# Depthwise convolution by spectra over tokens, with the way back in plain float32

## The chip, the cores and the metric

The kernel runs on one core of a Trainium2 chip. What counts is the device time of one execution in microseconds (us). The engines are PE (TensorE, matrix products into PSUM), DVE (VectorE), ACT (ScalarE), POOL (GpSimd) and SP (SyncE, whose queue here issues every DMA). A line number such as L288 is a line of the kernel file.

## The reference

Two transformer blocks on 256 tokens of 1024 features in float32. The change touches one layer of the second block only, the conformer convolution:

```python
def conformer_conv(h, w_pw1, b_pw1, w_dw, b_dw, ln_g, ln_b, w_pw2, b_pw2):
    u = h @ w_pw1 + b_pw1                 # 256x1024 by 1024x2048
    a, gate = jnp.split(u, 2, axis=-1)
    u = a * jax.nn.sigmoid(gate)
    u = causal_dwconv_2(u, w_dw, b_dw)    # 31 taps over tokens, each feature by itself
    u = jax.nn.silu(layernorm(u, ln_g, ln_b))
    return u @ w_pw2 + b_pw2              # 1024x1024
# second_block: h = rmsnorm_2(x, ...);  x = x + conformer_conv(h, ...)
```

## The kernel before

All weights stream from DRAM in blocks of 128 x 1024 floats (0.52 MB). `chunk` loads one into a `raw` buffer (5 of them, SP's queue), ACT copies it to a rounded `hi` part (L335), and DVE subtracts that for a `lo` part (L336; 7 buffers of each). A product of full precision is three products of parts, high by high, high by low and low by high. `mm_b` does this with features on PSUM's partitions and 256 tokens as columns; `mm_a` with 128 tokens on the partitions and features as columns. `mm` (L288) is the one line behind all of them, so names of tiles tell products apart. Plain float32 products go through the same `mm`.

A framework with tile pools puts the semaphores and the order in which each engine takes its work; in this stage the order of steps is written out by hand in a string (`CONV_ORDER`).

The stage runs thus. The 256 tokens stand along columns, the features on partitions. `up_pair("pw1", j)` makes for each of 8 feature tiles the value and the gate half of the first pointwise layer, 16 blocks, 384 products of 256 columns (`ps_pw`). `glu` scales by the input's norm (`rsb`), adds biases, and writes `u` with 31 columns of zeros ahead (`upad`). Of the 31 taps some are multiply-adds on DVE (`conv_dve`, L948, 66 of them). The others run on PE: `conv_rows` sends the rows out to DRAM (`far`, L953) and reads them back with four shifted copies over the partitions (`ur`, L957), POOL builds diagonal matrices from the taps (`dw`), and `conv_pe` makes 184 products of 32 output rows (`pcv`). `PW_PE` says how many of eight groups of taps PE takes for each tile. Mean and variance over features are products with a matrix of ones (`pmu`, `pvar`, `pmd`), then the rest of the norm, SiLU, the split into parts, and the second pointwise layer (`pw`, 8 blocks, 192 products). The gated feed-forward behind it begins with `ps_up`.

The norm of the stage's input comes in the middle of the first products: `nm.row` sums squares with three products (`ssa`, `ssb`) and gives `rsb`. `tok_col` turns such a row into a column of scales by token (`ps_col`).

Of the kernel before, what the change touches and what calls it, by code (L numbers as in the profile page):

```python
# [56 lines left out]
def _plan():  # L57
# [87 lines left out]
def _dve_taps():  # L145

    return [(j, k) for j in range(8) for k in range(31) if (k + 1) % 8 >= PW_PE[j]]


def _rows4(w):  # L150

    w = np.concatenate([np.zeros_like(w[:1]), w], axis=0).reshape(4, 8, 8, 4, 32)
    return w.transpose(0, 4, 2, 1, 3).reshape(P, 256)
# [12 lines left out]
def _w2(w):  # L166
# [20 lines left out]
    ("b_pw1", 16, lambda I: _col(I["conv_b_pw1_2"], 16)),  # L187
    ("w_dw", 256, lambda I: _rows4(I["conv_w_dw_2"][0])),
    ("w_dv", len(_dve_taps()), lambda I: _taps(I["conv_w_dw_2"][0], 8)[:, [31 * j + k for j, k in _dve_taps()]]),
    ("b_dw", 8, lambda I: _col(I["conv_b_dw_2"], 8)),  # L190
# [18 lines left out]
def _offsets(items):  # L209
    o, out = 0, {}  # L210
    for name, n, *_ in items:
# [8 lines left out]
         ("cos", T), ("sin", T), ("cmpadd", 64), ("cmpmul", 64), ("eye4", 32), ("sbmask", P), ("cmask", P)]  # L220
# [46 lines left out]
def kernel(ctx: ExitStack, tc: tile.TileContext, x: bass.AP, mem: bass.AP, stream: bass.AP,  # L267
# [653 lines left out]
    yc = apool.tile([P, ND, T], F32, tag="b8", name="yc")  # L921
    NH = 31
    dve_taps = _dve_taps()

    def glu(j, ps):

        rt(rs)
        ag = spool.tile([P, 2, T], F32, tag="t2", name="ag", bufs=NT2)
        dve.tensor_mul(ag, ps, rb(rs))
        sg = spool.tile([P, T], F32, tag="t1", name="sg", bufs=NT1)  # L930
        fn(sg, ag[:, 1, :], AF.Sigmoid, bias=vec("b_pw1", 8 + j))
        up = spool.tile([P, NH + T], F32, tag="t1", name="upad", bufs=NT1)
        pool.memset(up[:, 0:NH], 0.0)
        dve.scalar_tensor_tensor(up[:, NH:], ag[:, 0, :], vec("b_pw1", j), sg, op0=ALU.add, op1=ALU.mult)
        return up

    def conv_dve(*js):

        first = {j: max([t for t in dve_taps if t[0] == j], default=None) for j in js}
        for k in range(30, -1, -1):  # L940
            for j in js:
                if (j, k) not in dve_taps:
                    continue
                w, u = vec("w_dv", dve_taps.index((j, k))), ups[j][:, k + 1:k + 1 + T]
                if (j, k) == first[j]:
                    act.activation(yc[:, j, :], u, AF.Identity, scale=w, bias=vec("b_dw", j))
                else:
                    dve.scalar_tensor_tensor(yc[:, j, :], u, w, yc[:, j, :], op0=ALU.mult, op1=ALU.add)  # L948

    def conv_rows(up):  # L950

        far = dpool.tile([P, NH + T], F32, tag="far", name="far")
        nc.sync.dma_start(far, up)  # L953
        r = apool.tile([P, 4, T + 7], F32, tag="c4", name="ur", bufs=NC4)
        for b in range(4):
            f = far[32 * b:32 * b + 32]
            nc.sync.dma_start(r[:, b, :], bass.AP(f.tensor, f.offset, [[8, 4], [NH + T, 32], [1, T + 7]]))  # L957
        return r

    def conv_pe(j):  # L960

        ps = acc_bank([P, T], "pcv")
        n = PW_PE[j]
        d = wpool.tile([P, 8, 4, 32], F32, tag="lo", name="dw", bufs=7)
        src = vec("w_dw", 32 * j, 4 * n).rearrange("p (g b) -> p g b", b=4)
        pool.tensor_mul(d[:, :n], src[:, :, :, None].to_broadcast([P, n, 4, 32]),
                        con("eye4")[:, None, None, :].to_broadcast([P, n, 4, 32]))
        for g in range(n):
            for b in range(4):
                mm(ps[32 * b:32 * b + 32, :], d[:, g, b, :], uss[j][:, b, g:g + T], g == 0, g == n - 1)  # L970
        return ps

    def conv_sum(j, ps):
        if PW_PE[j] == 8:
            act.activation(yc[:, j, :], ps, AF.Identity, bias=vec("b_dw", j))
        else:
            dve.tensor_add(yc[:, j, :], ps, yc[:, j, :])


    ups, uss, pcs, pss, w4, ln = {}, {}, {}, {}, [], {}  # L980

    def conv_mean():
        pmu = ms_bank([P, T], "pmu")
        m = spool.tile([P, T], F32, tag="t1", name="yp", bufs=NT1)
        pool.tensor_add(m, yc[:, 0, :], yc[:, 1, :])
        for i, y in enumerate((m, yc[:, 2, :], yc[:, 3, :])):
            mm(pmu, ones, y, i == 0, i == 2)
        ln["mu"] = spool.tile([P, T], F32, tag="t1", name="mu", bufs=NT1)
        act.activation(ln["mu"], pmu, AF.Copy, scale=1.0 / (4 * P))
        ln["var"], ln["md"] = up_bank([P, T], "pvar"), ms_bank([P, T], "pmd")  # L990

    def deviate(p):
        s = slice(2 * p, 2 * p + 2)
        dve.tensor_sub(yc[:, s, :], yc[:, s, :], rb(ln["mu"]))

    def moments(js):
        sq = spool.tile([P, 2, T], F32, tag="t2", name="sq", bufs=NT2)
        act.activation(sq[:, 0:len(js), :], yc[:, js[0]:js[-1] + 1, :], AF.Square)
        y = yc[:, js[0], :]
        if len(js) == 2:  # L1000
            pool.tensor_add(sq[:, 0, :], sq[:, 0, :], sq[:, 1, :])
            if js[0] == 4:
                y = spool.tile([P, T], F32, tag="t1", name="yp", bufs=NT1)
                pool.tensor_add(y, yc[:, 4, :], yc[:, 5, :])
        if js[0] >= 4:
            mm(ln["md"], ones, y, js[0] == 4, js[0] == 7)
        mm(ln["var"], ones, sq[:, 0, :], js[0] == 0, js[0] == 7)

    dve_groups = ((0, 1), (2, 4), (3, 5), (6, 7))

    steps = {
        "P": lambda j: pss.update({j: up_pair("pw1", j, xs, nm.row if j == PW_ORDER[1] else None)}),
        "G": lambda j: ups.update({j: glu(j, pss[j])}),
        "S": lambda j: PW_PE[j] and uss.update({j: conv_rows(ups[j])}),
        "E": lambda j: PW_PE[j] and pcs.update({j: conv_pe(j)}),
        "A": lambda j: PW_PE[j] and conv_sum(j, pcs[j]),
        "D": lambda j: conv_dve(*dve_groups[j]),
        "w": lambda j: w4.append(chunk(("pw2", j), D)),
        "m": lambda j: conv_mean(),
        "d": deviate,  # L1020
        "M": lambda j: moments((j,) if j > 5 else (j, j + 1)),
    }
    for step in CONV_ORDER.split():
        steps[step[0]](int(step[1]))
    m2 = spool.tile([P, T], F32, tag="t1", name="m2", bufs=NT1)
    act.activation(m2, ln["md"], AF.Square, scale=1.0 / math.sqrt(D))
    md = spool.tile([P, T], F32, tag="t1", name="md", bufs=NT1)
    dve.tensor_scalar(md, ln["md"], 1.0 / D, None, op0=ALU.mult)
    dve.tensor_sub(m2, ln["var"], m2)
    rl = rs_of(m2, D, eps2, "rl")  # L1030
    ys = pair_tile("x", bufs=2)
    acc = Acc("pw2")
    for p in range(4):
        s = slice(2 * p, 2 * p + 2)
        dve.tensor_sub(yc[:, s, :], yc[:, s, :], rb(md))
        dve.tensor_mul(yc[:, s, :], yc[:, s, :], rb(rl))
        for f in (2 * p, 2 * p + 1):
            fn(yc[:, f, :], yc[:, f, :], AF.Silu, scale=vec("ln_g", f), bias=vec("ln_b", f))
        for f in (2 * p, 2 * p + 1):
            split(ys, (slice(None), f), yc[:, f, :])  # L1040
        if p < 2:
            acc.add(("pw2", 2 * p), ys, 2 * p, w4[2 * p:2 * p + 2])
# [402 lines left out]
```

## Time and profile before

| | us |
|---|---|
| median of 3 runs | 1069.94 (1069.94, 1071.75, 1069.94) |
| the profiled execution | 1071.3 |
| its span, first to last instruction | 1069.5 |
| PE busy | 1035.4 (97%) |
| DVE busy | 734.8 (69%) |
| ACT busy | 579.7 (54%) |
| POOL busy | 60.2 (6%) |

All rows are from the one profiled execution. Its own time is 1.8 us over the span, and 1.4 us over the median. The mean granted clock of PE was 0.988 of full speed (2.4 GHz).

### The profile page before, as it was taken

To read this page: it belongs to the slowest core of one execution; us is meant where nothing else is said; L and a number is where in the kernel's file an instruction comes from. 1 tells how busy PE (TensorE), PEld (TensorE's weight loads), DVE (VectorE), ACT (ScalarE), POOL (GpSimd) and SP (SyncE) were. 2 spreads that over 40 slices of the span, in tenths; PEclk is the share of its full clock that TensorE was granted. 3 is DMA by queue.
4 is the path that set the end of the run, shared out by engine and by line. 5 is a ranking of instruction groups with operands and counts; after the bars stand their busy time and mean duration, and the time that the engine had idled before them with its cause. 6 is when DMAs were issued, how large, how long until landed. Compare 5 with 4: busy or idle time off the path is not lost.

```text
span 1069.5 us, 20182 instructions
## 1 busy us (share of the span) xinstructions
PE 1035.4 (97%) x8113; PEld 957.5 (90%) x8113; DVE 734.8 (69%) x1163; ACT 579.7 (54%) x968; POOL 60.2 (6%) x148
## 2 busy tenths in 40 slices
PE   7999999999999999778999999999999999999998
PEld 6998898999999999537999999998786799999997
DVE  5976568745545587955876677766887468667673
ACT  5766657644444473215654555553867656555551
POOL 0000000000000000320000000000124300000000
PEclk9999999999999999879999999999999999999999
DMA  8753234355655655352555555644742045656641
GB/s 307 241 182 119 79 119 157 131 186 176 195 182 173 195 168 155 96 165 76 186 187 179 181 189 167 197 156 139 226 139 60 2 126 190 199 177 196 182 154 40
DMA packets 52813, 170.43 MB, mean 159 GB/s; under 512 B 5744, under 2 KB 13168, under 8 KB 52720
## 3 DMA queue, kind: packets, MB, share of 16 engines
q1 hardware_dynamic: 51952, 168.09, 48.8%
q8 instruction: 64, 1.05, 0.4%
q0 software_dynamic: 768, 1.05, 0.4%
q14 instruction: 29, 0.24, 0.1%
HBM read 165.99 MB, written 2.08 MB: 157 GB/s over the span
## 4 chain that ended last, share of the span: by engine, by line
PE 87%; DMA 6%; DVE 5%; ACT 1%; issue 1%; SPq 0%; DVEq 0%; ACTq 0%
PE ps_up L288 23%; PE ff L288 9%; PE ps_ff L288 8%; PE ob L288 6%; PE dn L288 6%; PE ps_v L288 3%; PE nl L288 2%; PE pw L288 2%; PE ps_qk L288 2%; PE no L288 2%; PE wo L288 2%; DMA far<-upad 2%; PE npo L288 2%; DVE yc L948 2%; PE ps_nq L288 2%; DMA ur<-far 2%
## 5 line engine op out<-in xcount | busy, mean ns | idle before, releaser
L336 DVE TENSOR_TENSOR lo<-raw,hi 128x1024 fp32r<-128x1024 f32 x296 | 358.2, 1223 | 169.1 <-ACT hi L335 157.3
L335 ACT ACTIVATE hi<-raw 128x1024 fp32r<-128x1024 f32 x296 | 305.2, 1049 | 261.6 <-PE ps_up L288 62.9
L288 PE MATMUL ps_up<-xh,hi 128*128 128x256 f32 x704 | 199.6, 284 | 0.3 <-DVE fv L1057 0.3
L288 PE MATMUL ps_up<-xl,hi 128*128 128x256 f32 x704 | 199.5, 283 | 0.0
L288 PE MATMUL ps_up<-xh,lo 128*128 128x256 f32 x704 | 199.2, 283 | 0.0
L288 PEld LDWEIGHTS ps_up<-xh,hi 128*128 128x128 f32 x704 | 135.1, 192 | 0.9 <-DVE fv L1057 0.5
L288 PEld LDWEIGHTS ps_up<-xl,hi 128*128 128x128 f32 x704 | 135.1, 192 | 0.4
L288 PEld LDWEIGHTS ps_up<-xh,lo 128*128 128x128 f32 x704 | 135.1, 192 | 0.0
L288 PE MATMUL ff<-us,hi 128*128 128x256 f32 x512 | 92.8, 283 | 0.0
L288 PEld LDWEIGHTS ff<-us,hi 128*128 128x128 f32 x512 | 79.4, 190 | 0.2
L288 PE MATMUL ps_ff<-xh,hi 128*128 128x256 f32 x256 | 72.7, 284 | 0.2 <-DVE fr L871 0.2
L288 PE MATMUL ps_ff<-xl,hi 128*128 128x256 f32 x256 | 72.4, 283 | 0.0
L288 PE MATMUL ps_ff<-xh,lo 128*128 128x256 f32 x256 | 72.4, 283 | 0.0
L288 PE MATMUL ff<-us,lo 128*128 128x256 f32 x256 | 72.1, 282 | 0.0
L288 PE MATMUL dn<-us,hi 128*128 128x256 f32 x352 | 63.5, 282 | 0.0
L288 PE MATMUL ob<-hi,us 128*128 128x512 f32 x176 | 56.2, 392 | 0.0
L288 PEld LDWEIGHTS dn<-us,hi 128*128 128x128 f32 x352 | 54.6, 191 | 0.0
L288 PE MATMUL dn<-us,lo 128*128 128x256 f32 x176 | 49.7, 282 | 0.0
L288 PEld LDWEIGHTS ps_ff<-xh,hi 128*128 128x128 f32 x256 | 49.1, 192 | 0.4 <-PE ps_ff L288 0.4
L288 PEld LDWEIGHTS ps_ff<-xl,hi 128*128 128x128 f32 x256 | 49.1, 192 | 0.0
L288 PEld LDWEIGHTS ps_ff<-xh,lo 128*128 128x128 f32 x256 | 49.1, 192 | 0.0
L288 PEld LDWEIGHTS ff<-us,lo 128*128 128x128 f32 x256 | 48.7, 190 | 0.0
(417 smaller groups left out, 2394.6 us busy)
## 6 DMA issues: line engine op xcount, KB each, us to landing
raw<-in_stream_dram SPq DMA_DIRECT2D x302, 512.0 KB
ur<-far SPq DMA_DIRECT2D x28, 131.5 KB
xin<-in_mem_dram SPq DMA_DIRECT2D x4, 256.0 KB
xin<-in_x_dram SPq DMA_DIRECT2D x4, 256.0 KB
out_dram<-htok SPq DMA_DIRECT2D x4, 256.0 KB
far<-upad SPq DMA_DIRECT2D x7, 143.5 KB
ct<-in_cons_dram SPq DMA_DIRECT2D x1, 720.0 KB
vt<-in_vecs_dram SPq DMA_DIRECT2D x1, 539.0 KB
```

The source lines that it names most:

```text
L288: pe.matmul(ps, l, r, start=start, stop=stop, skip_group_check=True, **kw)
L335: act.activation(hi[:, :width], raw[:, :width], AF.Copy)
L336: dve.tensor_sub(lo[:, :width], raw[:, :width], hi[:, :width].bitcast(F32))
L948: dve.scalar_tensor_tensor(yc[:, j, :], u, w, yc[:, j, :], op0=ALU.mult, op1=ALU.add)
```

## The change

Only the convolution stage changes, up to the products `pw`; those and all that follows are as before. Tokens now lie on the partitions. The first layer is four projections of 512 features (`g0`, `a0`, `g1`, `a1`: gate and value, first and second half), each of four blocks and 48 products of 512 columns (`mm_a`). The biases come as rows broadcast over the partitions by DMA (`bb`, two buffers). The convolution is done in blocks of 128 tokens by a real DFT of length 160: 36 products of parts with a table (`ps_f`), a multiplication with the spectrum of the taps on DVE (`sq`), and 8 plain float32 products back (`ps_y`). The tap spectra are four float32 products with 32 rows (`ps_sp`). The table and the taps are loaded into two of the five `raw` buffers. The layer norm is bn_stats and bn_aggr by token, Ln and Exp for the reciprocal root, one scaling on ACT and one on DVE for each half of the tokens, 16 transposes back to features (`ps_t`), and SiLU. The scratch in DRAM (`far`) is gone, the vectors shrink from 1078 to 727 columns, and the constants lose a small identity.

```diff
@@ the weight stream @@
-    for j in PW_ORDER:
-        both("pw1", "conv_w_pw1_2", 0, j, D)
+    add(("dft", 0), 1024, lambda I: _dft())
+    add(("taps", 0), 256, ...)
+    add(("b_pw1", 0), 16, ...)
+    for b in range(2):
+        wide(("g", b), D + 512 * b)
+        wide(("a", b), 512 * b)
@@ the stage @@
-    glu, conv_dve, conv_rows, conv_pe, conv_sum, conv_mean, deviate, moments
-    for step in CONV_ORDER.split():
-        steps[step[0]](int(step[1]))
-    m2, md, rl, and yc = (yc - md) * rl on DVE
+    def dft_load():
+        raw, _ = raw_chunk(("dft", 0))
...
+        taps = wpool.tile([P, 1024], F32, tag="raw", name="taps", bufs=5)
...
+    def tap_spectra(m):
+        for b in range(2):
+            s = slice(512 * b, 512 * b + 512)
+            ps = (up_bank, ms_bank)[m]([P, 512], "ps_sp")
+            mm(ps, cv["raw"][0:32, 768 + P * m:768 + P * m + P], cv["taps"][0:32, s], True, True)
+            act.activation(cv["v"][:, m, s], ps, AF.Copy)
+    def project(key):
+        kind, b = key
+        cv[key] = ps = [acc_bank([P, 512], "ps_pw%d" % t) for t in range(2)]
+        cv["b", key] = bb = spool.tile([P, 512], F32, tag="bb", name="bb", bufs=2)
...
+        for k in range(4):
+            w = chunk((key, k), 512)
+            for t in range(2):
+                for kt in range(2):
+                    mm_a(ps[t], xs, 2 * k + kt, slice(P * t, P * t + P), w, kt, slice(None), ...)
+            if key == ("g", 0) and k == 2:
+                nm.row()
+    def biased(key, t):     # DVE: (projection * token scale) + bias row
+    def gates_of(b):        # ACT: sigmoid of both biased halves
+    def glu(b):             # value * gate, split into parts u.h, u.l
+    def forward(b, t, banks):
...
+        for m in range(2):
+            ps = banks([P, 512], "ps_f")
+            for k in range(t + 1):
+                fh, fl = (p_[:, m] for p_ in cv["f"][k])
+                mm(ps, fh, u.h[:, t - k, s], k == 0, False)
+                mm(ps, fh, u.l[:, t - k, s], False, False)
+                mm(ps, fl, u.h[:, t - k, s], False, k == t)
+            q = apool.tile([P, 512], F32, tag="c4", name="sq", bufs=NC4)
+            dve.scalar_tensor_tensor(q, ps, con("pad")[:, m:m + 1], cv["v"][:, m, s], op0=ALU.add, op1=ALU.mult)
+    def back(b, t, banks):
+        cv["y", b, t] = ps = banks([P, 512], "ps_y")
+        for m in range(2):
+            mm(ps, cv["g"][:, m], cv["q", b, t, m], m == 0, m == 1)
...
+        dve.bn_stats(cv["st", t][:, b, :], ps)
+    def normed(t):          # bn_aggr, Ln, Exp, then the scaling: b = 0 on ACT, b = 1 on DVE
+    def feature(p, t):      # two transposes of 128x128 into ps_t
+    def activated(p):       # SiLU with gain and bias, split
+    project(("g", 0)); dft_load(); gates_of(0); project(("a", 0))
+    tap_spectra(0); tap_spectra(1); glu(0)
+    project(("g", 1)); gates_of(1); project(("a", 1)); glu(1)
+    w4 = [chunk(("pw2", j), D) for j in range(2)]
+    forward(0, 0), forward(0, 1), forward(1, 0), back(0, 0), forward(1, 1),
+    back(1, 0), back(0, 1), normed(0), back(1, 1)
+    w4 += [chunk(("pw2", j), D) for j in range(2, 4)]
+    feature(p, 0) for four p; normed(1); feature(p, 1), activated(p) for four p
```

PE at the end of the convolution before, from the last of `ps_pw` to the first of `pw` (`pcv` the taps on PE, `pmu`, `pvar` and `pmd` the sums of the layer norm):

```order
L288 MATMUL ps_pw_4908<-xh,lo 128x256
L288 MATMUL pcv<-ur,dw 32x256 x152
L288 MATMUL pmu<-yp,ct 128x256
L288 MATMUL pmu<-yc,ct 128x256 x2
L288 MATMUL pcv<-ur,dw 32x256 x32
L288 MATMUL pvar<-sq,ct 128x256 x2
...
L288 MATMUL pw_5338<-xh,hi 128x256
```

The same place after:

```order
L309 MATMUL ps_f<-xh,dfth 128x512
L309 MATMUL ps_f<-xl,dfth 128x512
L309 MATMUL ps_y<-sq,ginv 128x512 x2
L309 MATMUL ps_f<-xh,dftl 128x512
...
L309 MATMUL ps_y<-sq,ginv 128x512 x6
L1051 MATMUL ps_t<-ct,yn 128x128 x16
L309 MATMUL pw_4927<-xh,hi 128x256
```

The taps on PE and the sums are gone. The way back stands between and behind the forward products, and 16 transposes stand ahead of `pw`.

DVE in the middle of the stage before (`ag` the scaled product, `yc` the taps, `upad` the gated value):

```order
L929 TENSOR_TENSOR ag<-ps_pw_4716,rsb 128x512
L948 SCALAR_TENSOR_TENSOR yc<-upad,vt,yc 128x256 x3
L934 SCALAR_TENSOR_TENSOR upad<-ag,vt,sg 128x256
L948 SCALAR_TENSOR_TENSOR yc<-upad,vt,yc 128x256 x9
L929 TENSOR_TENSOR ag<-ps_pw_4847,rsb 128x512
L948 SCALAR_TENSOR_TENSOR yc<-upad,vt,yc 128x256 x13
```

DVE after, from the last gate to the second bn_stats (`pw` a biased projection, `sq` the spectral product, `lo` a weight split, `xl` the split of `u`):

```order
L989 SCALAR_TENSOR_TENSOR pw<-ps_pw_4586,col,bb 128x512
L357 TENSOR_TENSOR lo<-raw,hi 128x1024 x4
L989 SCALAR_TENSOR_TENSOR pw<-ps_pw_4667,col,bb 128x512
L989 SCALAR_TENSOR_TENSOR pw<-ps_pw_4668,col,bb 128x512
L1003 TENSOR_TENSOR pw<-pw 128x512 x2
L1018 SCALAR_TENSOR_TENSOR sq<-ps_f,ct,spec 128x512
L445 TENSOR_TENSOR xl<-pw,xh 128x512 x2
L1018 SCALAR_TENSOR_TENSOR sq<-ps_f,ct,spec 128x512 x5
L1027 BN_STATS bst<-ps_y 128x6
L357 TENSOR_TENSOR lo<-raw,hi 128x1024
L1018 SCALAR_TENSOR_TENSOR sq<-ps_f,ct,spec 128x512 x2
L357 TENSOR_TENSOR lo<-raw,hi 128x1024
```

Four weight splits in a row stand ahead of the last two biased projections, and only two more among the eight spectral products.

SP's queue after, from the last small block of the start to the end of the stage (`raw` weight blocks, `bb` bias rows; before, there are 117 loads of `raw` in a row from the same place on, and then the stores and loads of `far` and `ur`):

```order
L348 DMA raw<-in_stream_dram 128x64
L348 DMA raw<-in_stream_dram 128x1024 x2
L975 DMA bb<-in_stream_dram 128x512
L348 DMA raw<-in_stream_dram 128x1024
L975 DMA bb<-in_stream_dram 128x512
L348 DMA raw<-in_stream_dram 128x1024 x104
L949 DMA taps<-in_stream_dram 32x1024
L348 DMA raw<-in_stream_dram 128x1024 x8
L975 DMA bb<-in_stream_dram 128x512
L348 DMA raw<-in_stream_dram 128x1024 x3
L975 DMA bb<-in_stream_dram 128x512
L348 DMA raw<-in_stream_dram 128x1024 x81
```

The first two loads of bias rows stand among the first weight blocks of the program, the other two between blocks of the stage itself.

## Rows read from the trace of the kernel before

**Rows 1.** The page of the profiled execution: the span, each engine's busy time, share and count of instructions, PE's busy share in 40 equal slices of the span (9 is 90% or more), and the shares of the chain of work that ended last, by engine and then by line.

```profile
span 1069.5 us, 20182 instructions
PE 1035.4 (97%) x8113; PEld 957.5 (90%) x8113; DVE 734.8 (69%) x1163; ACT 579.7 (54%) x968; POOL 60.2 (6%) x148
...
PE   7999999999999999778999999999999999999998
...
PE 87%; DMA 6%; DVE 5%; ACT 1%; issue 1%; SPq 0%; DVEq 0%; ACTq 0%
PE ps_up L288 23%; PE ff L288 9%; PE ps_ff L288 8%; PE ob L288 6%; PE dn L288 6%; PE ps_v L288 3%; PE nl L288 2%; PE pw L288 2%; PE ps_qk L288 2%; PE no L288 2%; PE wo L288 2%; DMA far<-upad 2%; PE npo L288 2%; DVE yc L948 2%; PE ps_nq L288 2%; DMA ur<-far 2%
```

**Rows 2.** Timeline of PE where the convolution stage begins. Columns: start (us), duration (us), engine, line, operation, output and inputs, tile and shape, count.

```profile
383.64 0.28 PE L288 MATMUL ps_pw<-xh,hi 128*128 128x256 f32 x1
383.76 0.28 PE L288 MATMUL ps_pw<-xl,hi 128*128 128x256 f32 x1
```

**Rows 3.** The chain of waits in order of time, 380 to 520 us. Columns: start (us), duration (us), engine, what it did, line, count.

```profile
413.71 12.37 DMA far<-upad
...
466.43 9.30 DMA ur<-far
...
490.25 0.82 PE pw L288 x4
...
515.25 4.80 PE ps_up L288 x40
```

**Rows 4.** Busy time of each engine in stretches of 10 us. Columns: stretch, its length, then busy us and instructions of PE, PE's weight loads, DVE, ACT and POOL, the granted clock, the DMA engines' share, GB/s.

```profile
385.00:395.00 10.00, 10.00 (x80) 9.80 (x80) 10.00 (x16) 9.32 (x16) 0.13 (x1) 1.00 0.61 198
395.00:405.00 10.00, 9.05 (x75) 8.82 (x74) 9.76 (x17) 7.53 (x12) 0.12 (x1) 1.00 0.78 252
...
425.00:435.00 10.00, 5.55 (x33) 5.38 (x32) 8.83 (x14) 2.96 (x5) 4.62 (x5) 0.72 0.41 113
...
445.00:455.00 10.00, 5.79 (x74) 2.70 (x70) 10.00 (x13) 1.79 (x2) 5.13 (x6) 0.91 0.24 73
...
465.00:475.00 10.00, 6.49 (x65) 3.01 (x54) 4.53 (x6) 3.78 (x6) 3.09 (x4) 0.93 0.75 176
```

**Rows 5.** Groups of instructions by line and shape, 385 to 520 us. Columns: line, engine, operation, output and inputs, shapes, count | busy us, mean ns of one | idle us before them, and what ended it.

```profile
L948 DVE SCALAR_TENSOR_TENSOR yc<-upad,vt,yc 128x256 f32<-128x256 f32 x66 | 31.5, 528 | 0.1
L288 PE MATMUL pcv<-ur,dw 128*32 128x256 f32 x368 | 30.6, 448 | 10.4 <-DMA ur<-far 10.4
```

**Rows 6.** Timeline of PE in a later stage whose products have 512 columns; columns as in rows 2.

```profile
904.81 0.39 PE L288 MATMUL ob<-lo,us 128*128 128x512 f32 x1
905.03 0.62 PE L288 MATMUL ob<-hi,us 128*128 128x512 f32 x2
905.49 0.39 PE L288 MATMUL ob<-lo,us 128*128 128x512 f32 x1
```

**Rows 7.** Timelines of PE and of ACT at the norm of the stage's input; columns as in rows 2.

```profile
394.85 0.59 PE L288 MATMUL ssb<-sq,ct 128*128 128x256 f32 x2
...
396.21 0.42 ACT L389 ACTIVATE rsb<-rsb 128x256 f32<-128x256 f32 x1
```

**Rows 8.** The chain of waits in order of time, 0 to 110 us; columns as in rows 3. The products of `ps_v` are those of an early projection, `ps_col` is the token scale there, `ps_t` are 16 transposes and `seg` two float32 products of 512 columns in two pairs.

```profile
11.74 8.37 PE ps_v L288 x51
...
21.85 0.53 PE ps_col L288 x4
...
26.53 1.75 PE ps_t L536 x16
...
75.01 1.72 PE seg L288 x4
```

**Rows 9.** Timeline of PE at a float32 product that stands alone, in the attention stage; columns as in rows 2.

```profile
754.98 1.12 PE L288 MATMUL rot<-qraw,ct 128*128 128x512 f32 x2
756.04 0.33 PE L1153 MATMUL pt<-ct,hc 60*128 60x60 f32 x2
```

**Rows 10.** Timeline of ACT where the norm of the convolution stage ends; columns as in rows 2.

```profile
487.07 0.42 ACT L389 ACTIVATE rl<-rl 128x256 f32<-128x256 f32 x1
487.50 1.28 ACT L385 ACT_TABLE_LOAD   x1
488.80 1.09 ACT L389 ACTIVATE yc<-yc,vt 128x256 f32<-128x256 f32 x2
489.80 0.71 ACT L423 ACTIVATE xh<-yc 128x256 fp32r<-128x256 f32 x2
```

**Rows 11.** Groups of instructions by line and shape over the whole span, DVE and then ACT; columns as in rows 5.

```profile
L336 DVE TENSOR_TENSOR lo<-raw,hi 128x1024 fp32r<-128x1024 f32 x294 | 357.4, 1229 | 169.1 <-ACT hi L335 157.3 <-PE pcv L288 11.6
...
L1255 DVE TENSOR_REDUCE nnm<-nl 128x2 f32<-128x512 f32 x16 | 10.9, 687 | 3.9 <-PE nl L288 3.9
...
L1099 DVE SCALAR_TENSOR_TENSOR qraw<-qraw,gq,hsq 128x512 f32<-128x512 f32 x4 | 3.0, 749 | 0.0
...
L335 ACT ACTIVATE hi<-raw 128x1024 fp32r<-128x1024 f32 x294 | 304.5, 1054 | 261.6 <-PE ps_up L288 62.9 <-PE ff L288 45.1 <-PE ps_ff L288 42.0
```

**Rows 12.** Timeline of PE at the first products of `pw` (the idle time before them in brackets), and the busy time in the stretch behind; columns as in rows 2 and 4.

```profile
490.25 0.82 PE L288 MATMUL pw<-xh,hi 128*128 128x256 f32 x4 [4.58 <-ACT xh L423]
...
491.00:494.00 3.00, 2.97 (x14) 2.90 (x14) 2.23 (x7) 3.00 (x8) 0.00 (x0) 0.50 0.00 0
```

**Rows 13.** Waits of SP's own queue, 383 to 516 us. Columns: who waited for whom: us in total, times, longest us.

```profile
SPq L327 <- DVE lo L336: 70.9, 16, 16.4
```

More of the change, by code (lines that the diff above doesn't have):

```diff
@@ L107, in ffn, with wide @@
         downs("dn%d" % lay, "ffn_w_down_2", (NF2 - 2, NF2 - 1), lay)
-    for j in PW_ORDER:
-        both("pw1", "conv_w_pw1_2", 0, j, D)
+    def wide(key, c):
+        for k in range(4):
+            add((key, k), 1024, lambda I, k=k: _up(I["conv_w_pw1_2"][0][256 * k:256 * k + 256], c, c + 512))
+    add(("dft", 0), 1024, lambda I: _dft())
+    add(("taps", 0), 256, lambda I: np.concatenate([I["conv_w_dw_2"][0], I["conv_b_dw_2"]], axis=0).reshape(P, 256))
+    add(("b_pw1", 0), 16, lambda I: I["conv_b_pw1_2"][0].reshape(P, 16))
+    for b in range(2):
+        wide(("g", b), D + 512 * b)
+        wide(("a", b), 512 * b)
     downs("pw2", "conv_w_pw2_2", range(8))
@@ L142, in _taps, with _dft, spectra, forth @@
     return w.T.reshape(n, P, k).transpose(1, 0, 2).reshape(P, n * k)
[L145 to L153, printed above, removed]
+def _dft():
+    n, rows = 160, 256
+    ang = 2 * np.pi / n * np.arange(n)
+    def spectra(p, turn):
+        m = np.zeros((len(p), rows))
+        for f in range(1, 80):
+            c, s = np.cos(ang[f * p % n]), np.sin(ang[f * p % n])
+            for i, col in enumerate(turn(c, s)):
+                m[:, 3 * (f - 1) + i] = col
+        m[:, 237], m[:, 238] = 1.0, (-1.0) ** p
+        return m
+    def forth(c, s):
+        return c - s, c, -s
+    fm = spectra(32 + np.arange(P), forth)
+    fh = np.zeros((P, rows))
+    fh[96:] = spectra(np.arange(32), forth)
+    g = spectra(32 + np.arange(P), lambda c, s: (2 * (c - s), -2 * s, -2 * c)) / n
+    g[:, 255] = 1.0
+    kw = np.zeros((P, rows))
+    kw[:31] = spectra(30 - np.arange(31), lambda c, s: (c, -s - c, c - s))
+    kw[31, 255] = 1.0
+    g = g.T.reshape(2, P, P).transpose(1, 0, 2).reshape(P, 256)
+    return np.concatenate([fm, fh, g, kw], axis=1)
 def _top(v, n):
@@ L186 @@
     ("g_f1", 8, lambda I: _col(I["ffn_norm_g_2"][1], 8)),
[L187 to L190, printed above, removed]
     ("ln_g", 8, lambda I: _col(I["conv_ln_g_2"], 8)),
@@ L918 @@
     xs, rs = nm.xs, nm
[L921 to L1022, printed above, removed]
@@ L1023 @@
-    for step in CONV_ORDER.split():
-        steps[step[0]](int(step[1]))
[L1025 to L1030, printed above, removed]
+    cv = {}
+    def dft_load():
+        raw, _ = raw_chunk(("dft", 0))
+        off = offs["taps", 0][0]
+        taps = wpool.tile([P, 1024], F32, tag="raw", name="taps", bufs=5)
+        nc.sync.dma_start(taps[0:32], stream[off:off + 32 * D].rearrange("(p c) -> p c", p=32))
+        hi = wpool.tile([P, 1024], F32R, tag="hi", name="dfth", bufs=7)
+        lo = wpool.tile([P, 1024], F32R, tag="lo", name="dftl", bufs=7)
+        act.activation(hi[:, :512], raw[:, :512], AF.Copy)
+        dve.tensor_sub(lo[:, :512], raw[:, :512], hi[:, :512].bitcast(F32))
+        parts = [t_[:, :512].rearrange("p (k m n) -> p k m n", k=2, m=2) for t_ in (hi, lo)]
+        cv["f"] = [[p_[:, k] for p_ in parts] for k in range(2)]
+        cv["g"] = spool.tile([P, 2, P], F32, tag="rs", name="ginv", bufs=3)
+        act.activation(cv["g"], raw[:, 512:768].rearrange("p (m n) -> p m n", m=2), AF.Copy)
+        cv["v"] = apool.tile([P, 2, D], F32, tag="b8", name="spec")
+        cv["raw"], cv["taps"] = raw, taps
@@ new lines, in tap_spectra @@
+    def tap_spectra(m):
[8 more added lines that the diff above has]
+        cv["b", key] = bb = spool.tile([P, 512], F32, tag="bb", name="bb", bufs=2)
+        off = offs["b_pw1", 0][0] + 512 * b + D * (kind == "g")
+        row = stream[off:off + 512]
+        nc.sync.dma_start(bb, bass.AP(row.tensor, row.offset, [[0, P], [1, 512]]))
+        for k in range(4):
+            w = chunk((key, k), 512)
+            for t in range(2):
+                for kt in range(2):
+                    mm_a(ps[t], xs, 2 * k + kt, slice(P * t, P * t + P), w, kt, slice(None),
+                         k == 0 and kt == 0, k == 3 and kt == 1)
+            if key == ("g", 0) and k == 2:
+                nm.row()
+        if key == ("g", 0):
+            cv["col"] = tok_col(nm)
@@ new lines, in biased @@
+    def biased(key, t):
+        y = spool.tile([P, 512], F32, tag="t2", name="pw", bufs=NT2)
+        dve.scalar_tensor_tensor(y, cv[key][t], cv["col"][:, t:t + 1], cv["b", key], op0=ALU.mult, op1=ALU.add)
+        return y
+    def gates_of(b):
+        cv["s", b] = [biased(("g", b), t) for t in range(2)]
+        for s in cv["s", b]:
+            fn(s, s, AF.Sigmoid)
+    def glu(b):
+        if not b:
+            ut = pair_tile("x", bufs=2)
+            cv["u"] = W(*[p_.rearrange("p (t a) c -> p t (a c)", t=2) for p_ in (ut.h, ut.l)])
+        for t in range(2):
+            y = biased(("a", b), t)
+            dve.tensor_mul(y, y, cv["s", b][t])
+            split(cv["u"], (slice(None), t, slice(512 * b, 512 * b + 512)), y)
@@ new lines, in forward @@
+    def forward(b, t, banks):
+        s = slice(512 * b, 512 * b + 512)
+        u = cv["u"]
+        for m in range(2):
[7 more added lines that the diff above has]
+            dve.scalar_tensor_tensor(q, ps, con("pad")[:, m:m + 1], cv["v"][:, m, s], op0=ALU.add, op1=ALU.mult)
+            cv["q", b, t, m] = q
@@ new lines, in back @@
+    def back(b, t, banks):
+        cv["y", b, t] = ps = banks([P, 512], "ps_y")
+        for m in range(2):
+            mm(ps, cv["g"][:, m], cv["q", b, t, m], m == 0, m == 1)
+        if not b:
+            cv["st", t] = spool.tile([P, 2, 6], F32, tag="bst", name="bst")
+        dve.bn_stats(cv["st", t][:, b, :], ps)
+    def normed(t):
+        mv = spool.tile([P, 2], F32, tag="bmv", name="bmv")
+        dve.bn_aggr(mv, cv["st", t])
+        r = spool.tile([P, 2], F32, tag="brs", name="brs")
+        fn(r[:, 0:1], mv[:, 1:2], AF.Ln, bias=eps2)
+        fn(r[:, 0:1], r[:, 0:1], AF.Exp, scale=-0.5)
+        dve.scalar_tensor_tensor(r[:, 1:2], mv[:, 0:1], -1.0, r[:, 0:1], op0=ALU.mult, op1=ALU.mult)
+        for b in range(2):
+            y = spool.tile([P, 512], F32, tag="t2", name="yn", bufs=NT2)
+            if b:
+                dve.tensor_scalar(y, cv["y", b, t], mv[:, 0:1], r[:, 0:1], op0=ALU.subtract, op1=ALU.mult)
+            else:
+                act.activation(y, cv["y", b, t], AF.Identity, scale=r[:, 0:1], bias=r[:, 1:2])
+            cv["n", b, t] = y
@@ new lines, in feature @@
+    def feature(p, t):
+        if not t:
+            cv["t", p] = (up_bank if p < 2 else acc_bank)([P, 2, T], "ps_t")
+        for i in range(2):
+            b, c = divmod(2 * p + i, 4)
+            pe.transpose(cv["t", p][:, i, P * t:P * t + P], cv["n", b, t][:, P * c:P * c + P], ident)
+    def activated(p):
+        y = spool.tile([P, 2, T], F32, tag="t2", name="ya", bufs=NT2)
+        for i in range(2):
+            f = 2 * p + i
+            fn(y[:, i, :], cv["t", p][:, i, :], AF.Silu, scale=vec("ln_g", f), bias=vec("ln_b", f))
+            split(ys, (slice(None), f), y[:, i, :])
@@ new lines @@
+    project(("g", 0))
+    dft_load()
+    gates_of(0)
+    project(("a", 0))
+    for m in range(2):
+        tap_spectra(m)
+    glu(0)
+    project(("g", 1))
+    gates_of(1)
+    project(("a", 1))
+    glu(1)
+    w4 = [chunk(("pw2", j), D) for j in range(2)]
+    forward(0, 0, acc_bank)
+    forward(0, 1, up_bank)
+    forward(1, 0, acc_bank)
+    back(0, 0, up_bank)
+    forward(1, 1, acc_bank)
+    back(1, 0, up_bank)
+    back(0, 1, ms_bank)
+    normed(0)
+    back(1, 1, ms_bank)
+    w4 += [chunk(("pw2", j), D) for j in range(2, 4)]
@@ L1031 @@
+    for p in range(4):
+        feature(p, 0)
+    normed(1)
     ys = pair_tile("x", bufs=2)
+    for p in range(4):
+        feature(p, 1)
+        activated(p)
     acc = Acc("pw2")
[L1033 to L1042, printed above, removed]
+    for p in range(2):
+        acc.add(("pw2", 2 * p), ys, 2 * p, w4[2 * p:2 * p + 2])
```

8 lines of the change are left out of this document (2 added, 6 removed).

## The prediction

> **What bounds the kernel now.** Read the page first [rows 1]: TensorE (PE) is busy 97% of the span and makes 87% of the chain that ended last, so a change pays only where PE's time, or a wait of PE, goes away. The two DMA entries of that chain, `far<-upad` and `ur<-far`, belong to one place, the conformer convolution, and the slices show PE's one long sag there. So the second view is that stage by itself. Its first product (`ps_pw`) starts at 383.64 [rows 2], the first product of the second pointwise layer (`pw`) at 490.25, and the feed-forward after it (`ps_up`) at 515.25 [rows 3]: 106.6 us up to `pw`, 25.0 us of `pw`, 131.6 in all, of 1069.5. The chain of waits there names what the 106.6 us are: rows of `u` that go out to DRAM and come back (12.37 and 9.30 us the longest), DVE taps and products of 32 columns between them, then the layer norm by hand up to `pw`. The table by stretches says the same: PE is full or nearly so at first (10.00 and 9.05 of 10), then has 5.55, 5.79 and 6.49 busy in three later stretches, and the clock is 0.72 to 0.93 there [rows 4]. Of the 106.6 us the pointwise products are 384 at 0.12 [rows 2] = 46.1. The other 60 are convolution, norm and waits.
>
> **What goes.** All of these 60 us: 66 tap operations of DVE (31.5 us), 368 PE instructions `pcv` (30.6 us) [rows 5], the round trip through DRAM, POOL's diagonal matrices, the sums for mean and variance. DVE was busy for 8.83 and 10.00 of 10 us in two of these [rows 4], so its release counts as well. None of it lies beside other long work: the stage before and the one behind wait for it.
>
> **What comes, on PE.** The new order is one row of products without a DRAM trip. (a) Pointwise: 192 products of 512 columns for 384 of 256. The rows for 512 columns step by 0.68 per three [rows 6], 0.227 each: 192 x 0.227 = 43.6 us. (b) Three sums of the input norm, at about 0.5 [rows 7], 1.5; the token scale (`ps_col`) 0.5 [rows 8]. Its input comes 1.8 us after the last sum starts (394.85 to 396.63, [rows 7]); the sum and six products placed between (1.9) cover that. (c) Tap spectra: 4 float32 products of 512 columns. In the trace one float32 product is two instructions. The nearest row is `seg`, two such products (x4) in 1.72 [rows 8], 0.86 each, 3.4 us; a lone one (`rot`, x2) takes 1.06 until the next starts [rows 9], so 3.4 to 4.2. (d) Forward: 36 x 0.227 = 8.2. (e) Back: 8 float32 products, 6.9 (up to 8.5). Three products of parts would have taken 8 x 0.68 = 5.4, so the plain ones cost 1.5 us of PE and spare ACT and DVE eight splits. Together 43.6 + 2.0 + 3.4 + 8.2 + 6.9 = 64.1 us.
>
> **What comes behind the last product back.** PE waits here: bn_stats, bn_aggr, Ln, Exp, a table load, one normalisation, transposes, two SiLU, one copy. Rows of the old norm price them [rows 10]: bn_stats, which has no row, 0.69 (between the 0.69 of a reduction that reads 512 per partition from PSUM and the 1.23 of a 1024-wide operation, [rows 11]; I take the first, since it reads the same 512 once), aggregate 0.2 (no row; it reads 12 values, at least nothing and at most the 0.69), Ln and Exp of one column 0.2 to 0.3 each (0.42 is the row for 256; 0.5 for both), load 1.28, normalise 0.6 (between 0.35 for 256 columns and 1.05 for 1024, [rows 11]), two transposes 0.2 (sixteen take 1.75, [rows 8]), two SiLU 1.1, copy 0.35, and some 0.5 for hand-overs: 5.4 us. The load is the only ACT step that nothing hides.
> The rows of the old load show 1.30 us from its start at 487.50 to the next activation at 488.80 [rows 10]. The Trainium skill ("ScalarE: Activation LUTs", What ACT_TABLE_LOAD costs) says that a switch costs a load and a drain, about 2.66 us in all. The trace shows no such drain here; by the page the tail would be 1.4 us longer.
>
> **The other engines.** DVE has to follow PE. Over the four projections it does eight 512-wide scalings of a product with its bias row, four multiplies with the gate and four splits. None of them stands ahead of a weight split that PE is about to need: the order puts the next blocks' `lo` before them. Between the last projection and the last product back, DVE has two scalings, two multiplies, two splits, eight spectral products (512 wide, with a column operand: 0.75 [rows 11], some 0.68 a step since neighbours overlap), two weight splits and three bn_stats, 1.4 + 1.2 + 1.2 + 5.4 + 2.3 + 2.0 = 13.5 us beside PE's 15.1: hidden with about 1 us to spare, and if a spectral product took 1.0 instead, 1 to 2 us would show. ACT has about 20 us of weight copies and 10 us of its own in the whole stage; hidden.
> SP's queue gets four loads of bias rows (`bb`, 0.25 MB), and the last two stand behind weights and wait until an earlier projection has been read. PE uses those rows only a projection (10.9 us) later, so this is free unless weight loads queued behind them come late. The first two move to the start of the kernel, where they add 0.5 MB before the first projections of the whole program; vecs shrinks by 0.18 MB. PE is on the chain without a DMA wait from 11.7 us on [rows 8], so I take 0, at most 1. The tables of the transform hold two of the five `raw` buffers until the tap spectra are done; PE needs a block of weights per 12 x 0.227 = 2.7 us, and a block costs 1.05 of ACT and 1.23 of DVE [rows 11], so three buffers should do.
> From `pw` on I change nothing: PE is idle for about 4.5 us before it in both kernels, the clock was 0.50 for 491 to 494 [rows 12], and 25.0 stays.
>
> **Sum.** To `pw`: 64.1 + 5.4 + 0.7 for some 20 hand-overs of 0.02 to 0.05 = 70.2 us for 106.6. That is 36.4 less. The profiled execution took 1071.3 (span 1069.5, and 1.8 around it): 1034.9. The median of the runs shown, 1069.94, is 1.4 under that execution, so I forecast **1033.5 us** for the median, 0.966 of before.
>
> **Rivals.**
> *Weights late.* With three raw buffers, and `bb` loads ahead of weights in SP's queue, PE waits at each of the three borders between projections for one block: 2.7 us each, 8.1 together, 1041.6. For it: 16 waits of SP for the buffer that a DVE split frees, 70.9 us [rows 13]. Against it: the splits run up to six blocks ahead in the new order, and DMA has moved 198 and 252 GB/s in two stretches of this stage [rows 4], where 0.52 MB per 2.7 us are 193. 13%.
> *DVE bounds the spectra and the norm.* If operations with a column operand that read PSUM take 1.0 us and bn_stats 1.2, DVE's 13.5 becomes 17.5, 2.4 over PE, and the tail grows 0.5 for bn_stats and 1.5 for its small operations: 1033.5 + 4.4 = 1037.9. 12%.
> *Quicker.* The gap before `pw` is cut by the eight transposes and the clock stays up, which takes back the slow products (16 at 0.21 instead of 0.12, [rows 2, 12], 1.5 us), and the table load falls beside bn_stats, 1.3 us: 1030.7. 6%.
> The page's rule on table switches is one more: as a mechanism here, ACT drains before the load of the SiLU set, PE waits for it, +1.4, 1034.9. It is borne out by no row; 2%, inside the range.
> *Slower than before.* The clock is the one mechanism with such a size. At the granted 0.50, the lower level of 1.2 GHz, 14 products of 256 columns fill 3 us [rows 12], 0.214 each for 0.12 [rows 2], so the price is 1.78 times. Then the 64.1 us become 1.78 x 64.1 = 114, `pw` 1.78 x 23 = 41 (192 at 0.12 are 23), with 6 of tail 161 for 131.6: 1071 + 30 = 1100. It decides from where 47 us of the stage's products (36.4 / 0.78) run at 1.2 GHz. Against it: the clock is 1.00 in the stretches where PE is fed and is lower only where PE waits or has just waited [rows 4, 12], and the new order has one such place. 2%.
> *It does not do what it says:* a wait of PE on something in the spectra of the same length as the DRAM trips, so nothing is gained. I find none in the order; 1%.
>
> **Chances.** Forecast 64% (1032 to 1037), the others as given. Faster 0.97, within 0.2% (2.1 us, about what a measurement tells from no change) 0.01, slower 0.02. The range takes in the quick case, DVE and half of the late weights: 1030 to 1041.
>
> **What would show it.** `ps_pw` of 512 columns stepping by 0.227 with no gap over 1 us to the tap spectra; from the first of them to `pw` 70 us (first `pw` near 454); PEclk 1.00 until the norm; no DMA on the chain in this stage; a gap of PE of 4 to 5.5 us before `pw`, ended by ACT. A gap ended by `lo<-raw` or by DMA speaks for late weights, gaps between `ps_f` and `ps_y` ended by DVE for the second rival. Wrong altogether if float32 products back step far over 1.06 us.

## The result and the profile after

The changed kernel took 1037.16 us (1036.58 to 1037.86, 4 runs) for 1069.94: a ratio of 0.9695, 95% interval 0.9683 to 0.9707, 32.8 us less. The forecast was 1033.5 with a range of 1030 to 1041. Timed again on another occasion the ratio was 0.9696 (0.9670 to 0.9721).

| | before | after |
|---|---|---|
| profiled execution, us | 1071.3 | 1037.86 |
| its span | 1069.5 | 1035.6 |
| first product of the stage to the first of `pw` | 106.6 | 71.9 |
| `pw` | 25.0 | 25.0 |
| first of `ps_up` to the end of the span | 554.3 | 554.8 |

The page of the profile after (as [rows 1]): PE's sag in the middle is gone but for one slice at 8, and so are the entries `far<-upad` and `ur<-far` of the chain.

```profile
span 1035.6 us, 19003 instructions
PE 1018.0 (98%) x7611; PEld 941.6 (91%) x7611; DVE 702.9 (68%) x1099; ACT 578.3 (56%) x963; POOL 43.2 (4%) x128
...
PE   7999999999999999989999999999999999999998
...
PE 93%; DVE 3%; DMA 2%; ACT 1%; issue 1%; SPq 0%; POOL 0%; DVEq 0%; ACTq 0%; POOLq 0%
PE ps_up L309 24%; PE ff L309 9%; PE ps_ff L309 8%; PE dn L309 6%; PE ob L309 6%; PE ps_pw L309 4%; PE ps_v L309 3%; PE nl L309 2%; PE pw L309 2%; PE ps_qk L309 2%; PE no L309 2%; PE wo L309 2%; PE npo L309 2%; PE ps_nq L309 2%; PE ps_xbc L309 2%; DVE lo L357 2%
```

The chain of waits through the stage after (columns as in [rows 3]; `bst`, `bmv`, `brs` and `yn` are the norm's statistics, their aggregate, the reciprocal root and the normalised value, L406 the table load, `ya` SiLU, `xh` the rounding copy):

```profile
384.08 8.19 PE ps_pw L309 x36
...
398.24 9.74 PE ps_pw L309 x42
407.98 3.62 PE ps_sp L309 x8
411.61 23.61 PE ps_pw L309 x96
435.22 5.89 PE ps_f L309 x26
441.11 1.72 PE ps_y L309 x4
442.83 2.32 PE ps_f L309 x10
445.14 5.17 PE ps_y L309 x12
...
450.33 0.71 DVE bst L1027
451.06 0.22 DVE bmv L1032
451.31 0.30 ACT brs L410
451.63 0.20 ACT brs L410
451.86 1.28 ACT L406
453.15 0.79 ACT yn L1042
453.98 0.45 PE ps_t L1051 x2
454.46 1.02 ACT ya L410 x2
455.48 0.31 ACT xh L444
455.83 25.01 PE pw L309 x192
480.84 8.28 PE ps_up L309 x69
```

Against [rows 3]: no DMA, and up to 450.3 nothing but PE. Then one chain through DVE and ACT to `pw`, step by step the one that the prediction listed. PE itself stands idle in it for 2.65 us and for 0.76 us, before and behind the second eight transposes, both ended by ACT. One line doesn't fit: 96 products of 512 columns in 23.61 us are 0.246 each, where 0.227 was forecast [rows 6] and the 36 of the first line have it. The timeline of PE there (columns as in [rows 2]) shows which are slow:

```profile
407.91 3.69 PE L309 MATMUL ps_sp<-taps,raw 32*128 32x512 f32 x8
...
412.92 0.63 PE L309 MATMUL ps_pw<-lo,xh 128*128 128x512 f32 x1
413.34 0.63 PE L309 MATMUL ps_pw<-hi,xl 128*128 128x512 f32 x1
...
416.45 0.39 PE L309 MATMUL ps_pw<-hi,xl 128*128 128x512 f32 x1
416.67 0.39 PE L309 MATMUL ps_pw<-hi,xh 128*128 128x512 f32 x1
```

The table by stretches (columns as in [rows 4]) tells why:

```profile
408.00:412.00 4.00, 4.00 (x10) 1.74 (x11) 4.00 (x6) 3.58 (x7) 0.00 (x0) 1.00 0.76 188
412.00:414.00 2.00, 2.00 (x7) 1.57 (x6) 0.87 (x2) 0.57 (x2) 0.00 (x0) 0.53 0.75 283
414.00:416.00 2.00, 2.00 (x7) 1.52 (x7) 0.00 (x0) 0.00 (x0) 0.00 (x0) 0.61 0.98 381
416.00:418.00 2.00, 2.00 (x10) 1.65 (x9) 0.73 (x1) 1.06 (x1) 0.00 (x0) 1.00 0.93 375
```

PE is busy in every one, and the granted clock still falls to its lower level, behind the tap products (`ps_sp`). They have 32 rows, not 128: that is the 32 in their shape.

### The profile page after: what moved, and what is told of

Same layout as the page of the kernel before. It is cut to its first block, busy times and chain, and to the rows that moved or that the text cites. A ratio compares the mean times of both kernels' runs of the same rounds, so it can differ in the third digit from the quotient of the medians.

```text
span 1035.6 us, 19003 instructions
## 1 busy us (share of the span) xinstructions
PE 1018.0 (98%) x7611; PEld 941.6 (91%) x7611; DVE 702.9 (68%) x1099; ACT 578.3 (56%) x963; POOL 43.2 (4%) x128
## 3 DMA queue, kind: packets, MB, share of 16 engines
q0 software_dynamic: 768, 1.05, 0.4%
HBM read 163.73 MB, written 1.05 MB: 159 GB/s over the span
## 4 chain that ended last, share of the span: by engine, by line
PE 93%; DVE 3%; DMA 2%; ACT 1%; issue 1%; SPq 0%; POOL 0%; DVEq 0%; ACTq 0%; POOLq 0%
PE ps_up L309 24%; PE ff L309 9%; PE ps_ff L309 8%; PE dn L309 6%; PE ob L309 6%; PE ps_pw L309 4%; PE ps_v L309 3%; PE nl L309 2%; PE pw L309 2%; PE ps_qk L309 2%; PE no L309 2%; PE wo L309 2%; PE npo L309 2%; PE ps_nq L309 2%; PE ps_xbc L309 2%; DVE lo L357 2%
```

## Experiments

All are made from the changed kernel unless said otherwise. "To `pw`" is the time from the first product of the stage to the first of `pw`; it was 71.9 us in the profile above.

**1. The changed kernel again.**

> The changed kernel once more, beside the three others of this set. 1037.2 us; in the trace the clock falls to 0.50 behind the tap spectra (412 to 415.5 us) as in its first profile.

1036.34 us (1033.60 to 1038.29). The half on the clock was wrong: this execution had no dip, and 22.00 us for the 96 products:

```profile
407.87 3.63 PE ps_sp L309 x8
411.50 22.00 PE ps_pw L309 x96
```

To `pw` it took 70.3 us, the forecast's 70.2. So the dip comes in some executions and not in others, and one run without it shows nothing. `pw` itself was longer here, 25.97 us for 25.01, so that to the end of `pw` the two profiles differ by 0.6 us only (96.3 and 96.9).

**2. Tap products over 128 rows.**

```diff
+        pool.memset(taps[32:64], 0.0)
+        pool.memset(taps[64:P], 0.0)
...
-            mm(ps, cv["raw"][0:32, 768 + P * m:768 + P * m + P], cv["taps"][0:32, s], True, True)
+            mm(ps, cv["raw"][:, 768 + P * m:768 + P * m + P], cv["taps"][:, s], True, True)
```

> The tap spectra multiply all 128 rows (96 of them zeros) and not 32. Theory A: the clock fell behind them because only 32 of 128 rows worked for 3.7 us, though PE was busy all the time; with 128 rows it stays 1.00, the 96 products of the next two projections take 21.8 us for 23.6, and the time is 1.8 us less, 1035.4. Theory B: plain float32 products as such lower it, or something else in this place does; then nothing changes, 1037.2.

1035.13 us (1032.85 to 1037.02), clock 1.00, the 96 products in 21.77, to `pw` 70.2. That is what theory A expects, but experiment 1 had no dip either, and the two times overlap. It does not decide; experiment 5 tests it with a longer row.

**3. Tap products spread.**

```diff
+    def tap_spectra(m, bs=(0, 1)):
+        for b in bs:
...
+            if key == ("g", 1):
+                tap_spectra(k // 2, (k % 2,))
...
-    for m in range(2):
-        tap_spectra(m)
```

> The four tap products, 32 rows as before, stand one behind each weight block of the third projection and not in a row. Theory A with the time in a row deciding: the clock stays 1.00, but each lone product has its gap (0.2 us each at most), 1035.5 to 1036.5. If every such product lowers the clock by itself, it falls four times and the time is above 1037.2.

1036.94 us (1035.97 to 1037.20). The clock was 1.00 through the tap products and the projections behind them, but the gaps cost more than I allowed:

```profile
410.85 1.05 PE ps_sp L309 x2
411.90 2.94 PE ps_pw L309 x12
```

Alone, a tap product takes 1.05 for 0.91 in a row, and the twelve products behind it 2.94 for 12 x 0.227 = 2.72: 0.36 us at each of four places, 1.4 us in all. Spreading gives back most of the 1.8 us that a dip costs.

**4. The way back in three products of parts.** The alternative to the plain float32 that the change is named after. The table for the way back (`gh`, `gl`) is split into parts as well.

```diff
+            act.activation(qp[:, 0], q, AF.Copy)
+            dve.tensor_sub(qp[:, 1], q, qp[:, 0].bitcast(F32))
...
-            mm(ps, cv["g"][:, m], cv["q", b, t, m], m == 0, m == 1)
+            mm(ps, gh, q[:, 0], m == 0, False)
+            mm(ps, gh, q[:, 1], False, False)
+            mm(ps, gl, q[:, 0], False, m == 1)
```

> The way back as three products of parts and not one of float32. By the prediction's terms PE has 24 x 0.227 = 5.4 us for 6.9, but DVE gets eight splits of 0.64 (5.1 us) beside the 14 that it has in a stretch of 15: DVE then bounds the stretch, and the time is 2 to 4 us more, 1039 to 1041. Rival: the splits are hidden, and the time is 1.5 us less, 1035.7.

1039.85 us (1037.76 to 1041.76), 3.5 more than experiment 1 beside it. The chain now runs through DVE from the last projection to the norm (a few of its lines), and in 433 to 448 DVE is busy for 15.00 of 15 us while PE has 13.81:

```profile
440.13 1.80 DVE sp L1020 x3
441.93 1.32 DVE sq L1018 x2
...
457.43 24.70 PE pw L309 x192
```

```profile
433.00:448.00 15.00, 13.81 (x60) 10.56 (x59) 15.00 (x25) 7.36 (x11) 0.00 (x0) 1.00 0.11 39
```

The same stretch of the changed kernel, without a gap of PE:

```profile
433.00:448.00 15.00, 15.00 (x58) 10.54 (x57) 13.97 (x20) 4.01 (x5) 0.00 (x0) 1.00 0.33 105
```

So the plain products cost PE some 1.5 us (6.9 for 24 x 0.227 = 5.4, the second an estimate) and save 3.3 us on the path (first of `pw` at 457.43 for 454.12 in experiment 1, neither with a dip, both starting within 0.2 us of each other).

**5. Each tap product three times, with 32 and with 128 rows.** The loop `for _ in range(3):` around the product; the values stay. The second has the edit of experiment 2 too.

> Each tap product is made three times over, with 32 rows: 12 float32 products in a row, some 10.9 us for 3.6 (the same values). Theory A (few rows at work let the clock fall): the clock is 0.50 within or behind them in every case, and the time is 7.3 us and 1.8 to 4 us more. Theory B (it falls by chance of the moment, whatever the rows): 1.00 as in the second run of the changed kernel, 7.3 us more.

> The same three times over, but with all 128 rows. Theory A: clock 1.00, 7 to 7.5 us more than the changed kernel, no slow products behind. Theory C (float32 products as such): 0.50 as with 32 rows.

1048.57 and 1040.47 us (one run each). With 32 rows:

```profile
406.95 17.27 PE ps_sp L309 x24
424.23 23.55 PE ps_pw L309 x96
```

```profile
408.00:410.00 2.00, 2.00 (x7) 0.78 (x6) 2.00 (x3) 1.27 (x2) 0.00 (x0) 1.00 0.70 183
410.00:416.00 6.00, 6.00 (x9) 2.46 (x8) 1.85 (x3) 1.47 (x3) 0.00 (x0) 0.54 0.60 185
416.00:422.00 6.00, 6.00 (x8) 2.33 (x7) 0.00 (x0) 0.60 (x1) 0.00 (x0) 0.50 0.00 0
...
426.00:428.00 2.00, 2.00 (x7) 1.60 (x6) 0.00 (x0) 0.00 (x0) 0.00 (x0) 0.62 1.01 406
```

With 128 rows:

```profile
407.48 10.30 PE ps_sp L309 x24
417.78 21.77 PE ps_pw L309 x96
```

```profile
410.00:416.00 6.00, 6.00 (x16) 2.65 (x15) 2.37 (x4) 2.40 (x4) 0.00 (x0) 1.00 0.63 197
```

Same products, same columns, PE busy without a break in both: 17.27 us, at 0.50 after the first 3.5, against 10.30 at 1.00, and 1.8 us more behind. Theory A's forecast came. Theory C (float32 as such) falls: with 128 rows the clock stays up. B (chance alone, whatever the rows) is not excluded by the count, since there is one execution of each: of all profiles with the tap products in one row, three of five with 32 rows have a fall and none of three with 128 (experiments 2, 5 and 9). The length speaks against B: here the clock is low from 410 until 427, until behind the last of these products, where the short rows that dip have it low for some 3.4 us (the first profile) and 6.8 us (experiment 6). What decides whether a dip comes in the short row is not shown.

**6. SiLU left out, and its table load.** A scaling of the same width stands in its place.

```diff
-            fn(y[:, i, :], cv["t", p][:, i, :], AF.Silu, scale=..., bias=...)
+            act.activation(y[:, i, :], cv["t", p][:, i, :], AF.Identity, scale=..., bias=...)
```

> The SiLU behind the norm is left out (a scaling of the same width stands in its place), and with it the table load. Prediction's term: the load is the one step of ACT that nothing hides and costs its own 1.28 us, so the gap from the last product back to the first of pw falls from 5.5 to 4.2 us. By the drain that the page on tables adds, it would fall by 2.7, to 2.9. If other work ends the wait (DVE's half of the norm), it falls by less than 0.8.

1035.53 us (one run; what follows the stage works on other values). The gap from the last product back to `pw` fell from 5.5 to 4.5 us (450.93 to 455.38). The load is worth 1.1 of its 1.28: DVE's small operation for the norm, hidden by it before, now shows with 0.17 us. This execution had a dip as well, which cost 3 us. It came early: the tap products took 4.03 and the 96 behind them 24.78. With the shorter tail `pw` took less:

```profile
455.38 23.51 PE pw L309 x192
```

PE's idle pieces are 1.56 and 0.76 us here, and the clock is 1.00 from the tail through all of `pw`.

**7. The kernel before again.**

> The kernel before once more, for the spread of its profile. If its first profile is typical, the stage takes 106.6 us up to the first product of pw and 25.0 of pw, and what the forecast missed lies in the changed kernel. If its first profile was a slow one there (by 1 us or more), a part of the missing 3.6 us is the baseline's.

1069.05 us, span 1067.3. To `pw` 105.7 us (382.18 to 487.90) for 106.6, `pw` 24.87. So some 0.9 us of the stage in [rows 3] was that one execution's.

**8. Both kernels without the convolution.** After: tap products, `ps_f`, `sq`, `ps_y` left out, the norm reads the gated value; the tables are still loaded. Before: taps on DVE and PE and the trip through DRAM left out, likewise.

> The changed kernel without its convolution: taps, products forward and back and spectral products are left out, and the norm reads the gated value from SBUF. By the terms of the sum 3.4 + 8.2 + 6.9 = 18.5 us of PE go (1.8 more where the clock dips), and 2 to 3 us of DVE's scaling, gating and first statistics come to light behind the last projection: first product of pw 54 to 56 us after the first of the stage, for 70.3 to 71.9.

> The kernel before without its convolution: no taps on DVE or PE, no trip through DRAM; the norm reads the gated value. If the 60 us beside the pointwise products are the convolution and its waits, the stage up to pw falls from 106 to about 60 us (46.1 of products, 2 of the input's norm, 2 of gating, some 10 of the old norm): 46 us for the convolution before against 16 to 18 after. If the old norm was the larger part (over 20 us), it falls to 70 or more only.

1027.74 and 1030.94 us (one run each). To `pw`, after: 57.3 us (383.94 to 441.23), 1.3 over the upper end. Before: 64.9 (383.46 to 448.36), not 60. The part behind the last pointwise product (the last gate, then the norm) was larger than I took the old norm for:

```profile
397.48 34.69 PE ps_pw L288 x287
...
448.36 24.92 PE pw L288 x192
```

432.17 to 448.36 are 16.2 us. So, by what leaving it out saves, the convolution cost 41 to 42 us before and 13 to 15 after, and the rest (projections, gate, norm) 64.9 and 57.3. Only the stage is read from these two; what follows it worked on other values, and its clock differs (mean 0.992 and 0.997).

**9. PE kept busy in the tail, and 128 rows.** With the edit of experiment 2:

```diff
+    warm = acc_bank([P, 512], "warm")
+    for _ in range(3):
+        mm(warm, ones, ct[:, 0:512], True, True)
     normed(1)
...
         feature(p, 1)
+        if p == 3:
+            mm(warm[:, 0:256], ones, ct[:, 0:256], True, True)
```

> As the run with 128 rows, and PE makes float32 products of constants that nobody reads while it waits for the norm: three of 512 columns between the two sets of transposes, one of 256 before pw. Theory: pw takes 25.0 us for 192 x 0.12 = 23.0 because the clock falls in the idle tail; filled, the clock stays 1.00 and pw takes 23.0 to 23.4, so with the 128 rows the time is 3.5 us below the changed kernel, 1033.5. Rival: the filler delays the transposes (up to 0.5 us) and the clock falls all the same: 1035 to 1036.

1033.40 us (1032.79 to 1034.16), ratio 0.9659 (0.9640 to 0.9679): the lowest ratio of all. Its interval lies just below that of the changed kernel's first measurement (0.9683 to 0.9707) and overlaps that of experiment 1 (0.9670 to 0.9721) and of experiment 2 (0.9655 to 0.9710), so the times alone do not show what the filler adds to the 128 rows. The clock does: its mean is 0.999 to 1.000 in all five executions, 0.997 or 0.998 in all four of experiment 2, and 0.993 to 0.998 in all nine of the changed kernel. Its lines:

```profile
411.24 21.77 PE ps_pw L309 x96
...
453.62 23.51 PE pw L309 x192
```

`pw` takes 23.5 us for 25.0, and the clock is 1.00 in every stretch from 448 to 462. In all seven profiles with the full tail and no filler `pw` took longer, 24.03 to 25.97 us. In the first profile of the changed kernel the clock was 0.63 and 0.52 behind 456:

```profile
456.00:458.00 2.00, 2.00 (x11) 1.84 (x12) 1.24 (x4) 2.00 (x7) 0.00 (x0) 0.63 0.00 0
458.00:460.00 2.00, 2.00 (x11) 2.00 (x11) 0.85 (x3) 2.00 (x7) 0.00 (x0) 0.52 0.00 0
```

The filler does not delay the tail: 448.12 to 453.62 are 5.5 us, as without it.

## Why the prediction was right, and where its size was off

**The bound.** Right. The whole gain lies between the first product of the stage and `pw` (34.7 us between the first profiles, 33.8 to 36.3 with the second ones). What lies behind is as before within 0.5 us in the first profiles; in the second one of the changed kernel `pw` is 1.0 us longer. The median, 1037.16, is 0.16 above the 1032 to 1037 that the prediction gave 64%, and nearer to the 1037.9 of its DVE rival than to 1033.5; it is the traces, not the number, that tell the two apart.

**The sum on PE**, 64.1 us. Its terms, measured: 44.1 for 192 projections where there is no dip (22.06 and 22.00; forecast 43.6), 1.8 for the sums and the token scale (2.0), 3.6 for taps (3.4), 8.2 forward (8.2), 6.9 back (6.9): 64.6. The 0.7 for hand-overs between the products was not there (0.2 is left between 64.6, the tail's 5.5 and the 70.3 of experiment 1), so that the total came out at 70.3 for 70.2 by two small misses that cancel. The two loads moved to the start cost nothing that can be seen: the stage begins at 383.92 for 383.64, and the second profiles of the two kernels have 383.80 and 382.18.

**The tail**, 5.4 us: 5.5, with bn_stats 0.71 for 0.69, aggregate 0.22 for 0.2, Ln and Exp 0.50 for 0.5, a normalisation of 0.79 for 0.6, two transposes of 0.45 for 0.2, and hand-overs of some 0.25 for 0.5. The activation before the load ends at 451.83, the load takes 451.86 to 453.14, and the next activation starts at 453.15; without the load the gap was 1.1 us shorter (experiment 6). The Trainium skill ("ScalarE: Activation LUTs", What ACT_TABLE_LOAD costs) adds a drain to the load in every switch of tables. No such drain shows here. Two readings of the tail were wrong and cost nothing: the 0.35 for 256 columns stands in [rows 10] (two in 0.71), not in [rows 11], and PE is idle before `pw` for 3.4 us in two pieces, not in one gap of about 4.5 as before.

**DVE.** Right that it is hidden with about 1 us to spare: it is busy for 13.97 us of the 15 in 433 to 448, PE has no gap there, and a spectral product takes 0.74 (0.75 forecast). Experiment 4 shows what becomes of it with 5 us more. The rival in which DVE bounds did not occur; nor did late weights: the timeline has no idle time of PE from the first product of the stage to the last product back. The quick rival did not occur either: the load stays on the chain, and the clock falls behind the tail in every profile that has the full tail without filler.

**The step that was off**: the products of the second half at 0.227 each, and behind that the sentence that the clock is lower only where PE waits or has just waited. It also falls while PE is busy, behind products of 32 rows: this cost 1.8 us in the first profile (23.61 for 21.8), nothing in the second, 3 in experiment 6. The sign "PEclk 1.00 until the norm" failed with it. The clock rival asked for 47 us at the lower level; the falls of the changed kernel last a few us and come in a place that the prediction did not look at.

The miss of 3.66 us adds up from the first profiles: 0.3 ahead of the stage, 1.7 in it (71.9 for 70.2, which is the dip; the other terms cancel), 0.5 behind `pw`, 0.45 outside the span (2.26 for 1.8), and 0.7 from the base: the execution before was 1.4 over its median, which I carried over whole, the one after only 0.7. The second profile of the kernel before fits that, with 0.9 less in the stage. These tenths are those of single executions: over all occasions those of the kernel before lie between 1066.46 and 1073.33, those of the changed one between 1033.60 and 1038.29. How often a dip comes in the changed kernel is not settled: of four profiles with 32 rows in one short row two have it (the first and experiment 6) and two don't (experiments 1 and 4).

**The old parts.** That all the 60 us beside the pointwise products would go was right; how they divide was not in the prediction, and my guess in experiment 8 undersized the old norm with the last gate before it (16 us, not 10). The gain of 35 is some 27 from the convolution; of the other 8, some 2 are from wider products (44.1 for 46.1) and the rest from the norm and the gate.

## What to carry to other kernels

A step that makes DVE, DMA and PE wait for each other in turn can be worth replacing by more PE work, if that work runs in one row without waiting: price the new row by product durations, and the chain behind its last product one operation at a time. When choosing between plain float32 and products of parts, count the splits on the engine that is nearest to its limit, not only the products. Look at PE's clock also where PE is always busy: filling products of 32 rows up to 128 took 7 us off a long row of them here, and is not shown to pay for a short one. An idle tail may be worth filling or shortening, if what follows it is long: the filler took 1.5 us off `pw` here.

## What was not expected of the hardware

The granted clock fell to its lower level while PE was busy without a break, with products that use 32 of 128 rows: 0.54 and 0.50 in a row of twelve float32 products, 17.27 us for 10.30 with zeros in the other 96 rows at 1.00 (one run each). In the short row of four it does so in some executions only, and the slow products then stand mostly behind the row and not in it. A float32 product of 32 rows alone among products of parts cost about 0.36 us more than in a row of its kind (1.05 for 0.91, and 2.94 for 2.72 behind it).
